# S5 mixer: signs and decays made behind the scan, one transfer for a Toeplitz matrix, a norm factor in step order

## The chip, the cores and the metric

The program runs on one core of a Trainium2 chip. The metric is device time in microseconds (us) from the start to the end of one launch, the median of several runs; lower is better. TensorE is called PE below (PEld is its weight load), VectorE DVE, ScalarE ACT, GpSimd POOL, and SyncE, which issues all the transfers here, SP.

## The reference

The reference sends 256 tokens of 1024 features through two blocks in 32-bit floats. The first block has two layers: a mixer of a convolution and a retention, then a feed-forward part; and a second layer whose mixer is the bidirectional S5 that this change touches, then a feed-forward part. The second block is a mix of three attentions and a gated feed-forward part. Of the S5 mixer, this is what matters:

```python
def _mixer_s5(h, lam_re, ..., w_glu_a, w_glu_b):
    # 64 groups of 16 channels each drive a 64-dim complex diagonal state, per direction
    ug = u.reshape(bsz, seq, 64, 16)
    ...
    for direction in (0, 1):
        bu = einsum('sgc,gpc->sgp', us, bb[direction])              # complex
        h = associative_scan(_s5_combine, (a, bu), reverse=direction == 1)
        y = y + einsum('sgp,gcp->sgc', h_re, c_re) - einsum('sgp,gcp->sgc', h_im, c_im)
    y = y + d_skip * u
    z = gelu(y)
    return (z @ w_glu_a) * sigmoid(z @ w_glu_b)
```

The input `h` of the mixer is the root-mean-square norm of `x`, scaled and shifted by a modulation.

## The kernel before

Features lie on partitions and the 256 tokens in the free dimension. A dense layer takes its weights in pieces of 1 MB: `load` (L296) transfers a piece into one of four tiles of the tag `w`, `split` (L301) makes a high part of it on ACT (L314) and a low part on DVE (L315) into the tags `hi` and `lo` (two tiles each), and `lin` multiplies by three matmuls (L319 to L321). While the first layer's feed-forward part runs, `s5_tables` builds the S5 tables and writes them to memory: `Wd` (into the states), `Vd` (out of them) and `Kd` (a Toeplitz matrix of the taps inside a chunk).

The second layer's mixer begins with the norm: `rms` sums squares, takes the inverse root, and `spread` (L369) puts the factor of each token on all partitions, as two matmuls into PSUM. `modulated` (L1150 on DVE, L1151 on ACT) multiplies and shifts, and turns token order into step order: the 256 tokens are 32 chunks `j` of 8 steps `s`, stored as `(j s)`, and the stage wants `(s j)`.

`s5` then works on eight rows `ip` of eight groups each. For a row:

- `load(ip)` transfers `Wt` and `Vt` (two transfers of 512 KB each) and, for even rows, the Toeplitz matrix `Mt` (1 MB for two rows) as eight transfers of 16 partitions each (L1018). It also makes the small factors: `dm`, the decays with a zero at each chunk row's start (L1022 on POOL, L1026 on ACT), and `sg`, the signed sines (L1024, L1025 on ACT). The rooms that the tables use are borrowed: `wplace`, `vplace` and `mplace` name tags whose tiles the dense layers also use. `dm` and `sg` have two tiles each, so those of row `ip + 2` take the room of row `ip`.
- `chunk_states(ip)` multiplies the input by `Wt` on PE (L1039), copies the result `X` to SBUF on ACT (L1041) and transposes it on PE (L1045).
- `scan(ip)` has six operations on DVE: L1058, L1059 and L1060 turn the states, L1061 is the scan along the chunks with `dm`, L1065 and L1066 turn back; POOL adds the halves (L1067, L1068) into `S`.
- `outputs(ip)` adds up `Mt` (L1079) and `S` with `Vt` (L1081) on PE; after an odd row ACT copies the result to `Y` (L1114).

The loop has a look-ahead of two rows for the loads and of one row for the states:

```python
tabs = {ip: load(ip) for ip in range(self.ahead)}              # ahead = 2
pT = {ip: chunk_states(ip, tabs[ip]) for ip in range(self.skew)}  # skew = 1
for ip in range(8):
    if ip + self.ahead < 8:
        tabs[ip + self.ahead] = load(ip + self.ahead)
    if ip + self.skew < 8:
        pT[ip + self.skew] = chunk_states(ip + self.skew, tabs[ip + self.skew])
    S = scan(pT.pop(ip), tabs[ip])
    ...
    outputs(ip, S, tabs.pop(ip), pY)
```

`finish` adds the skip term (L1094), applies the activation (L1095) and splits the result; the two dense layers `glu_a` and `glu_b` follow, four pieces each. The low part of their first pieces (L315) is tied behind the last scan on DVE; the high part on ACT (L314) isn't tied to anything.

The order of instructions on each engine and on the transfer queue isn't the program's order. A planner makes it while the program is built: it goes by priority, which is program order, among what its own model of the times holds to be ready. On the chip each engine then runs its queue strictly in that order. `X`, `S` and the two products of L1065 and L1066 share one tag of five tiles, and a tile is handed on when its last reader is done.

Of the kernel before, what the change touches and what calls it, by code (L numbers as in the profile page):

```python
# [12 lines left out]
ALU = mybir.AluOpType  # L13
# [161 lines left out]
class K:  # L175
# [185 lines left out]
            st.add(x)  # L361
        return st.get()

    def spread(self, cols, tag=None):

        n = cols.shape[1]
        pb = self.ps(tag or self.pb_tag)[:, :128 * n]
        for b in range(n):
            self.nc.tensor.matmul(pb[:, 128 * b:128 * b + 128], cols[:, b:b + 1].to_broadcast([128, 128]), self.ident, start=True, stop=True)  # L369
        return pb  # L370

    def rms(self, x, st=None):

        ms = self.sumsq(x, st)
        return self.spread(self.rsqrt_eps(ms[:, :, 0]))

    def gained(self, x, g):

# [573 lines left out]
    def s5(self, x, u, fill, need, between, each, l=1):  # L952

        nc, v = self.nc, self.nc.vector

        H2 = self.sb([128, 16, 8, 16])
        for ih in range(2):
            for s4 in range(2):
# [3 lines left out]
                o = H2[:, 8 * ih:8 * ih + 8, 4 * (1 - s4):8 - 4 * s4][:, :, ::-1].rearrange("p i s c -> p s i c")  # L962
                src = ps.rearrange("p (s i c) -> p s i c", s=4, i=8)
# [6 lines left out]
        for i4 in range(4):  # L970
# [3 lines left out]
            o = U[:, 4 * i4:4 * i4 + 4].rearrange("p i x -> p (i x)")  # L974
# [6 lines left out]
        def tab(shape, tag):  # L981
            return self.tabs[tag].tile(shape, F32, name=self.name(tag), tag=tag)
# [11 lines left out]
        def wide(tag, place, ip):  # L994

            t = room(tag, place)
            src = self.Wd if tag == "Wt" else self.Vd
            out = []
            for i in range(2):
                o = t[:, 1024 * i:1024 * i + 1024]  # L1000
                nc.sync.dma_start(o, src[2 * ip + i].rearrange("p g n -> p (g n)"))
                out.append(o)
            return out
# [4 lines left out]
        mt = []  # L1008

        def load(ip):  # L1010
            Wt = wide("Wt", self.wplace[ip], ip)
            Wt = [w.rearrange("p (e r d q) -> p e r d q", e=4, r=2, d=2) for w in Wt]
            dm = tab([128, 2, 8, 32], "dm")
            if ip % 2 == 0:

                mt.append(room("Mt", self.mplace[ip // 2]).rearrange("p (l e i n) -> p l e i n", e=4, i=4, n=16))
                for s in range(8):
                    nc.sync.dma_start(mt[-1][16 * s:16 * s + 16].rearrange("c l e i n -> c (l e i n)"),  # L1018
                                      self.Kd[ip // 2][:, s:s + 8].rearrange("c l e n -> c (l e n)"))
            Mt = mt[-1][:, :, :, 2 * (ip % 2):2 * (ip % 2) + 2]  # L1020
            Et = self.E[:, :, 8 * ip:8 * ip + 8]
            nc.gpsimd.memset(dm[:, :, :, 0], 0.0)  # L1022
            sg = tab([128, 2, 8, 32], "sg")
            nc.scalar.copy(sg[:, 0], Et[:, 1])  # L1024
            nc.scalar.mul(sg[:, 1], Et[:, 1], -1.0)  # L1025
            (nc.scalar.copy if self.dm_act else nc.gpsimd.tensor_copy)(dm[:, :, :, 1:], self.rho[:, None, 8 * ip:8 * ip + 8, None].to_broadcast([128, 2, 8, 31]))  # L1026
            Vt = wide("Vt", self.vplace[ip], ip)
            Vt = [w.rearrange("p (e r n) -> p e r n", e=4, r=2) for w in Vt]
            return Wt, Vt, Mt, Et[:, 0], sg, dm

        def chunk_states(ip, tabs):

# [16 lines left out]
        Z, Tt = (self.ps(q).rearrange("p (r g j) -> p r g j", r=2, j=32) for q in ("fa", "fp"))  # L1049
        v.memset(Z[:, :, :, 0], 0.0)  # L1050

        def scan(pT, tabs):
            cs, sg, dm = tabs[3:]
            both = lambda a: a[:, None].to_broadcast([128, 2] + list(a.shape[1:]))

            t = [self.sb([128, 2, 8, 32], tag="q2") for _ in range(2)]
            a, b = t[0][:, :, :, 1:], t[1][:, :, :, 1:]
            tt(a, pT[:, :, :, 0:31], both(cs[:, :, 1:]), op=ALU.mult)  # L1058
            tt(b, pT[:, ::-1, :, 0:31], sg[:, :, :, 1:], op=ALU.mult)  # L1059
            tt(Z[:, :, :, 1:], a, b, op=ALU.add)  # L1060
            v.tensor_tensor_scan(fl(Tt), fl(dm), fl(Z), 0.0, op0=ALU.mult, op1=ALU.add)  # L1061
            S = self.sb([128, 2, 8, 32])
            fw, bw = slice(0, 64), slice(64, 128)
            t = [self.sb([128, 2, 8, 32]) for _ in range(2)]
            tt(t[0], Tt, both(cs), op=ALU.mult)  # L1065
            tt(t[1], Tt[:, ::-1], sg[:, ::-1], op=ALU.mult)  # L1066
            nc.gpsimd.tensor_tensor(S[fw], t[0][fw], t[1][fw], op=ALU.add)  # L1067
            nc.gpsimd.tensor_tensor(S[bw][:, :, :, ::-1], t[0][bw], t[1][bw], op=ALU.add)  # L1068
            return S

        def outputs(ip, S, tabs, pY):
            _, Vt, Mt = tabs[:3]
            for i in range(2):
                for k in range(3):
                    for e in range(4):
                        o = pY[32 * e:32 * e + 32, 2 * (ip % 2) + i]
                        kw = dict(start=k == 0, stop=k == 2, tile_position=(0, 32 * e))
                        if k == 0:
                            nc.tensor.matmul(o, U[:, 2 * ip + i, 32 * e:32 * e + 32], Mt[:, :, e, i], **kw)  # L1079
                        else:  # L1080
                            nc.tensor.matmul(o, S[:, k - 1, 4 * i + e], Vt[i][:, e, k - 1], **kw)  # L1081

# [16 lines left out]
        if self.warm:  # L1099
            nc.scalar.activation(self.sb([128, 1]), self.half, AF.Gelu_apprx_tanh)  # L1100
        tabs = {ip: load(ip) for ip in range(self.ahead)}
        pT = {ip: chunk_states(ip, tabs[ip]) for ip in range(self.skew)}
        for ip in range(8):
            if ip + self.ahead < 8:
                tabs[ip + self.ahead] = load(ip + self.ahead)
            if ip + self.skew < 8:
                pT[ip + self.skew] = chunk_states(ip + self.skew, tabs[ip + self.skew])
            S = scan(pT.pop(ip), tabs[ip])
            scanned = {mybir.EngineType.DVE: self.last(mybir.EngineType.DVE)}
            if ip % 2 == 0:  # L1110
                pY = self.ps(self.y_tag[ip // 2 % 2]).rearrange("p (i n) -> p i n", i=4)
            outputs(ip, S, tabs.pop(ip), pY)
            if ip % 2:
                nc.scalar.copy(Y[:, :, 2 * ip - 2:2 * ip + 2].rearrange("p t i c -> p i t c"), pY.rearrange("p i (t c) -> p i t c", c=16))  # L1114
            if ip == 3 + self.defer:
                with self.held(mybir.EngineType.DVE):
                    finish(0)
            self.behind(fill, self.rates[2][1])
# [7 lines left out]
        for j in range(4):  # L1126
            pa, pb = self.pair(), self.pair("fp")
# [10 lines left out]
            for c in range(2):  # L1138
                n = 2 * j + c
# [5 lines left out]
    def modulated(self, x, r, g, shift):  # L1145

        u = self.sb([128, 2, 8, 4, 32])
        for c in (0, 2, 4, 6, 1, 3, 5, 7):
            h, by = self.sb([128, 8, 32]), lambda a: a.rearrange("p (j s) -> p s j", s=8)
            self.nc.vector.scalar_tensor_tensor(h, by(x[:, c]), g[:, c:c + 1], by(r), op0=ALU.mult, op1=ALU.mult)  # L1150
            self.nc.scalar.activation(u[:, c % 2, :, c // 2], h, AF.Identity, bias=shift[:, c:c + 1])  # L1151
        return u

# [399 lines left out]
    def build(self, stop=None):  # L1553
        nc = self.nc
        with ExitStack() as es:
# [8 lines left out]
            x = self.keep([128, 8, T], "x")  # L1564
# [29 lines left out]
            with self.phase(s4=self.m4, ap=1, cv=self.ncv):  # L1594
                self.mark("norm0")
                h = self.normed(x, self.rms(x), self.modg(0, 1, 0), self.modv(0, 0))
                self.mark("mixer0")
                st = Sums(self)
# [8 lines left out]
            with self.phase(s4=4):  # L1607
                self.mark("norm0f")
                h = self.normed(x, self.rms(x, st), self.modg(0, 4, 1), self.modv(0, 3))
                self.mark("ffn0")  # L1610
                st = Sums(self)
# [8 lines left out]
            self.rate = self.rates[2]  # L1620
            with self.phase(s8=4):
                self.mark("norm1")
                u = self.modulated(x, self.rms(x, st), self.modg(1, 1, 0), self.modv(1, 0))
                self.mark("s5")
                def between():
                    nonlocal mem
                    tab_pools.close()
                    self.mkv, self.memh = mem_pools.enter_context(rpool("mkv", 1)), memh_pool.__enter__()
                    mem = Fill(self.memory())
                    ACT = mybir.EngineType.Activation  # L1630
                    self.after(mem, self.memat[0], ACT, self.last(ACT))

                mem, mem_pools, memh_pool = None, ExitStack(), rpool("memh", 1)
                st = Sums(self)
                self.s5(x, u, ada, lambda: need(1, 2), between, lambda j: st.add(x))
                need(1, 4)
                glu_end = self.last(mybir.EngineType.PE)
                self.dump("x3", x)
# [4 lines left out]
            with self.phase(s4=4):  # L1643
                self.mark("norm1f")
                r = self.rms(x, st)
                if self.mempace:
                    self.after(mem, self.memat[1], mybir.EngineType.PE, glu_end)
                h = self.normed(x, r, self.modg(1, 4, 1), self.modv(1, 3))
# [58 lines left out]
```

## Time and profile before

| | |
|---|---|
| median of 3 runs | 1232.63 us (1230.88 to 1236.48) |
| the profiled execution | 1235.0 us, of which its span 1233.2 us |
| busy share of the span | PE 95%, PEld 90%, DVE 72%, ACT 50%, POOL 8% |
| granted TensorE clock, mean | 0.971 of full speed |

A row of the timeline gives the start in us from the span's start, the duration, the engine (SPq is SP's queue), the line, the operation with its output and input, how many instructions were merged into it, and in brackets how long the engine had been idle before it and what released it. Buffer numbers are left out of names, so `s`, `at`, `fp` are all tiles of a tag. A transfer in SP's rows is its issue, not its movement.

### The profile page before, as it was taken

The page shows a single profiled execution, that of the slowest core. Times are in us where ns is not written, and L with a number is a line of the kernel's source. Part 1 is how long each engine was busy: PE and PEld are TensorE (multiplying, and loading weights), DVE is VectorE, ACT ScalarE, POOL GpSimd, SP SyncE. Part 2 cuts the span into 40 slices and gives each one's busy share as a digit, 9 for nine tenths or more (in the row PEclk, how much of TensorE's full clock was granted, in tenths as well). Part 3 has the DMA queues.
Part 4 walks back from the last instruction along what each step waited for, and adds up shares of the span by engine and source line. Part 5 has one row for each costly group of instructions (what it writes and reads, how often), then busy time and mean ns, then how long its engine had stood idle before and what let it go on. Part 6 is the DMA issues. An engine that isn't in the chain of part 4 may idle for free. (4 is left out here: it accounts for less than half of the span.)

```text
span 1233.2 us, 25410 instructions
## 1 busy us (share of the span) xinstructions
PE 1168.6 (95%) x10482; PEld 1110.2 (90%) x10482; DVE 890.2 (72%) x1813; ACT 613.5 (50%) x1218; POOL 104.0 (8%) x122
## 2 busy tenths in 40 slices
PE   6899897999999965799999999999999999999998
PEld 3688686999999954699999999999999999999998
DVE  7879887889888867766766656686666686666564
ACT  3577243655555643546444445573455545454441
POOL 0078321000000005100000000000000000000000
PEclk9899997999999978799999999999999999999999
DMA  9879886788888999354465655443454454555541
GB/s 348 337 304 334 295 293 200 236 271 286 284 295 269 297 274 343 123 186 162 159 262 206 223 187 167 167 171 103 137 172 137 152 173 157 187 187 172 193 157 60
DMA packets 64091, 267.29 MB, mean 217 GB/s; under 512 B 10196, under 2 KB 29028, under 8 KB 36840
## 3 DMA queue, kind: packets, MB, share of 16 engines
q1 hardware_dynamic: 63976, 265.68, 62.7%
q8 instruction: 82, 1.34, 0.4%
q14 instruction: 33, 0.27, 0.1%
HBM read 246.85 MB, written 18.81 MB: 215 GB/s over the span
## 5 line engine op out<-in xcount | busy, mean ns | idle before, releaser
L315 DVE TENSOR_TENSOR lo<-w,hi 128x512 fp32r<-128x512 f32 (+1 forms) x640 | 428.0, 714 | 148.7 <-ACT hi L314 148.1
L314 ACT ACTIVATE hi<-w 128x512 fp32r<-128x512 f32 (+1 forms) x640 | 358.3, 625 | 337.1 <-PE mm L320 120.1
L319 PE MATMUL mm<-h,hi 128*128 128x256 f32 x1328 | 380.9, 287 | 0.4 <-ACT h L398 0.3
L320 PE MATMUL mm<-h,hi 128*128 128x256 f32 x1328 | 378.8, 285 | 1.2 <-DVE h L399 1.1
L321 PE MATMUL mm<-h,lo 128*128 128x256 f32 x1328 | 379.9, 286 | 0.1
L319 PEld LDWEIGHTS mm<-h,hi 128*128 128x128 f32 x1328 | 256.0, 193 | 7.4 <-issue 3.4
L320 PEld LDWEIGHTS mm<-h,hi 128*128 128x128 f32 x1328 | 256.0, 193 | 2.8 <-DVE h L399 1.5
L321 PEld LDWEIGHTS mm<-h,lo 128*128 128x128 f32 x1328 | 255.8, 193 | 2.7 <-issue 1.6
L321 PE MATMUL at<-s,lo 128*128 128x256 f32 x720 | 204.4, 284 | 1.4 <-DVE lo L315 1.4
L319 PE MATMUL at<-s,hi 128*128 128x256 f32 x720 | 204.8, 284 | 0.0
L320 PE MATMUL at<-s,hi 128*128 128x256 f32 x720 | 204.1, 284 | 0.0
L321 PEld LDWEIGHTS at<-s,lo 128*128 128x128 f32 x720 | 137.9, 192 | 2.2 <-DVE lo L315 1.8
L319 PEld LDWEIGHTS at<-s,hi 128*128 128x128 f32 x720 | 138.0, 192 | 1.8 <-issue 1.4
L320 PEld LDWEIGHTS at<-s,hi 128*128 128x128 f32 x720 | 138.0, 192 | 0.6 <-issue 0.6
L439 PE MATMUL fa<-wa,crep 128*32 128x256 f32 x704 | 56.1, 424 | 6.9 <-DMA wa<-in_ada_dram 3.7
L537 POOL TENSOR_TENSOR s<-s,cv 128x256 f32<-128x256 f32 x60 | 49.9, 864 | 39.1 <-ACT cv L536 39.0
L439 PEld LDWEIGHTS fa<-wa,crep 128*32 128x32 f32 x704 | 22.6, 118 | 27.0 <-DMA wa<-in_ada_dram 5.9
L320 PE MATMUL fp<-h,hi 128*128 128x256 f32 x144 | 41.6, 289 | 0.9 <-DVE h L315 0.9
L319 PE MATMUL fp<-h,hi 128*128 128x256 f32 x144 | 41.4, 288 | 0.0
L321 PE MATMUL fp<-h,lo 128*128 128x256 f32 x144 | 41.4, 287 | 0.0
L929 ACT COPY Wt<-fp 128x512 f32<-128x512 f32 x32 | 18.6, 581 | 44.7 <-PE fp L928 41.2
L536 ACT ACTIVATE cv<-ap,s 128x256 f32<-128x256 f32 x60 | 29.5, 506 | 17.2 <-POOL s L537 16.4
(439 smaller groups left out, 1826.0 us busy)
## 6 DMA issues: line engine op xcount, KB each, us to landing
w<-in_fc_dram SPq DMA_DIRECT2D x64, 1024.0 KB, 5.0
wa<-in_ada_dram SPq DMA_DIRECT2D x44, 1024.0 KB, 6.6
w<-in_w_in_dram SPq DMA_DIRECT2D x38, 1024.0 KB, 4.9
w<-in_w_gate_dram SPq DMA_DIRECT2D x11, 1024.0 KB, 4.8
w<-in_w_up_dram SPq DMA_DIRECT2D x11, 1024.0 KB, 4.9
Vd<-V SPq DMA_DIRECT2D x16, 512.0 KB, 6.5
w<-in_w_out_dram SPq DMA_DIRECT2D x8, 1024.0 KB, 6.2
Wd<-Wt SPq DMA_DIRECT2D x16, 512.0 KB, 5.3
```

What stands on the lines that cost most here:

```text
L314: self.nc.scalar.activation(hi, h, AF.Copy)
L315: self.nc.vector.tensor_tensor(lo, h, hi.bitcast(F32), op=ALU.subtract)
L319: mm(ps, sh, mh, start=start, stop=False, skip_group_check=True)
L320: mm(ps, sh, ml, start=False, stop=False, skip_group_check=True)
L321: mm(ps, sl, mh, start=False, stop=stop, skip_group_check=True)
L439: nc.tensor.matmul(ps[32 * q:32 * q + 32], self.crep[:, 2 * k + k2], w[:, n:n + 256], start=k == 0 and k2 == 0, stop=k == 3 and k2 == 1, t ...
L536: nc.scalar.mul(t, src, w)
L537: nc.gpsimd.tensor_tensor(acc[:, ch], acc[:, ch], t, op=ALU.add)
L929: nc.scalar.copy(W[:, :, k], pt.rearrange("p (e x) -> p e x", e=4))
```

## The change

Three edits. First, `load(ip)` no longer makes `sg` and `dm`; a new function `factors(ip)` does, on the same engines. It is called for rows 0 and 1 ahead of the loop, and for row `ip + 2` right after `scan(ip)`, which is the last reader of the room that they take. Second, `Mt` is filled by one transfer on all 128 partitions in place of eight on 16 each; its source pattern has the dimensions step (8), channel (16) and run (2048 elements). Third, the norm's factor is put into PSUM in step order: the matmuls of `spread` write with a stride of 32 elements, and `modulated` reads it in a row, where it read it with a stride of 8 elements.

```diff
-    def spread(self, cols, tag=None):
+    def spread(self, cols, tag=None, steps=False):
...
-            self.nc.tensor.matmul(pb[:, 128 * b:128 * b + 128], cols[:, b:b + 1].to_broadcast([128, 128]), self.ident, start=True, stop=True)
+            o = pb.rearrange("p (s j) -> p j s", s=8)[:, 16 * b:16 * b + 16] if steps else pb[:, 128 * b:128 * b + 128]
+            self.nc.tensor.matmul(o, cols[:, b:b + 1].to_broadcast([128, 128]), self.ident, start=True, stop=True)
...
         def load(ip):
...
-            dm = tab([128, 2, 8, 32], "dm")
             if ip % 2 == 0:
...
-                for s in range(8):
-                    nc.sync.dma_start(mt[-1][16 * s:16 * s + 16].rearrange("c l e i n -> c (l e i n)"),
-                                      self.Kd[ip // 2][:, s:s + 8].rearrange("c l e n -> c (l e n)"))
+                src = self.Kd[ip // 2]
+                nc.sync.dma_start(mt[-1].rearrange("p l e i n -> p (l e i n)"),
+                                  bass.AP(tensor=src.tensor, offset=src.offset, ap=[[256, 8], [3840, 16], [1, 2048]]))
...
-            nc.gpsimd.memset(dm[:, :, :, 0], 0.0)
-            sg = tab([128, 2, 8, 32], "sg")
-            nc.scalar.copy(sg[:, 0], Et[:, 1])
-            nc.scalar.mul(sg[:, 1], Et[:, 1], -1.0)
-            (nc.scalar.copy if self.dm_act else nc.gpsimd.tensor_copy)(dm[:, :, :, 1:], self.rho[:, None, 8 * ip:8 * ip + 8, None].to_broadcast([128, 2, 8, 31]))
...
+        def factors(ip):
+
+            Et, rho = self.E[:, :, 8 * ip:8 * ip + 8], self.rho[:, None, 8 * ip:8 * ip + 8, None]
+            sg, dm = tab([128, 2, 8, 32], "sg"), tab([128, 2, 8, 32], "dm")
             nc.scalar.copy(sg[:, 0], Et[:, 1])
             nc.scalar.mul(sg[:, 1], Et[:, 1], -1.0)
+            nc.gpsimd.memset(dm[:, :, :, 0], 0.0)
+            nc.scalar.copy(dm[:, :, :, 1:], rho.to_broadcast([128, 2, 8, 31]))
+            return Et[:, 0], sg, dm
...
+        fac = {ip: factors(ip) for ip in range(2)}
...
-            S = scan(pT.pop(ip), tabs[ip])
+            S = scan(pT.pop(ip), fac.pop(ip))
...
+            if ip + 2 < 8:
+                fac[ip + 2] = factors(ip + 2)
             outputs(ip, S, tabs.pop(ip), pY)
...
-            self.nc.vector.scalar_tensor_tensor(h, by(x[:, c]), g[:, c:c + 1], by(r), op0=ALU.mult, op1=ALU.mult)
+            self.nc.vector.scalar_tensor_tensor(h, by(x[:, c]), g[:, c:c + 1], r.rearrange("p (s j) -> p s j", s=8), op0=ALU.mult, op1=ALU.mult)
...
-                u = self.modulated(x, self.rms(x, st), self.modg(1, 1, 0), self.modv(1, 0))
+                u = self.modulated(x, self.rms(x, st, True), self.modg(1, 1, 0), self.modv(1, 0))
```

## Rows read from the trace of the kernel before

**Rows 1.** Page, part 2: busy tenths of PE in 40 slices of the span.

```profile
PE   6899897999999965799999999999999999999998
```

**Rows 2.** Windows of the S5 stage: window, length, then busy time per engine, clock, DMA share, GB/s.

```profile
455.00:482.00 27.00, 18.65 (x416) 14.88 (x415) 24.10 (x33) 9.82 (x22) 13.05 (x15) 0.87 1.03 344
482.00:497.00 15.00, 4.53 (x69) 2.96 (x68) 6.97 (x10) 5.85 (x13) 4.49 (x4) 0.74 0.64 229
497.00:510.00 13.00, 8.23 (x146) 6.46 (x142) 12.76 (x25) 3.83 (x8) 5.40 (x4) 0.76 0.16 42
```

**Rows 3.** Timeline of DVE, rows 5 to 7 of the loop.

```profile
482.56 1.23 DVE L1061 TENSOR_TENSOR_SCAN fp<-dm,fa 128x512 f32<-128x512 f32 x1
...
486.75 1.23 DVE L1061 TENSOR_TENSOR_SCAN fp<-dm,fa 128x512 f32<-128x512 f32 x1
488.08 0.69 DVE L1065 TENSOR_TENSOR s<-fp,E 128x512 f32<-128x512 f32 x1
496.56 0.69 DVE L1066 TENSOR_TENSOR s<-fp,sg 128x512 f32<-128x512 f32 x1 [7.79 <-PE at L1045]
```

**Rows 4.** Timeline of PE, the same stretch.

```profile
475.16 2.08 PE L1039 MATMUL mm<-Wt,s 128*32 128x128 f32 x62
...
479.46 1.06 PE L1039 MATMUL mm<-Wt,s 128*32 128x128 f32 x32
...
495.34 1.11 PE L1045 MATMUL at<-ident,s 128*128 128x128 f32 x4 [8.22 <-ACT s L1041]
```

**Rows 5.** Timeline of ACT, the same stretch.

```profile
481.20 0.56 ACT L1041 COPY s<-mm 128x512 f32<-128x512 f32 x1
...
491.52 2.19 ACT L314 ACTIVATE hi<-w 128x512 fp32r<-128x512 f32 x4 [9.15 <-DMA w<-in_glu_a_dram]
493.61 0.59 ACT L1026 COPY dm<-rho 128x496 f32<-128x496 f32 x1
...
494.73 0.56 ACT L1041 COPY s<-mm 128x512 f32<-128x512 f32 x1
```

**Rows 6.** Timeline of SP's queue, end of the loop.

```profile
470.74 11.16 SPq L1018 DMA_DIRECT2D Mt<-Kd  x8
482.35 0.35 SPq L1216 DMA_DIRECT2D m<-in_mem_dram  x1
482.90 0.35 SPq L298 DMA_DIRECT2D w<-in_glu_a_dram  x1
```

**Rows 7.** Waits of SP from 415 to 520 us: total, times, longest.

```profile
SPq L1018 <- DMA Wt<-Wd: 10.5, 8, 2.7
```

**Rows 8.** Windows as in rows 2, by what the transfers carry.

```profile
478.00:484.00 6.00, 4.12 (x104) 3.28 (x108) 5.76 (x8) 2.96 (x7) 5.35 (x6) 1.00 0.96 194
464.00:478.00 14.00, 10.59 (x240) 8.56 (x232) 11.89 (x17) 4.82 (x11) 6.31 (x9) 0.83 1.04 409
426.00:432.00 6.00, 6.00 (x53) 6.00 (x52) 1.13 (x3) 1.50 (x3) 0.00 (x0) 1.00 1.06 161
```

**Rows 9.** By source line: issues of L1018 (ns), landings of L298 from 455 us.

```profile
L1018 SPq DMA_DIRECT2D Mt<-Kd x24: 302/318/932, 422.6 to 481.6; - x24
...
DMA to landing us min/median/max: 4.9/8.0/10.5
```

**Rows 10.** Waits of DVE from 455 to 503 us.

```profile
DVE q L1058 <- PE at L1045: 3.7, 3, 1.9
```

**Rows 11.** By source line: ns min/median/max, first and last start.

```profile
L1150 DVE SCALAR_TENSOR_TENSOR s<-x,modg,at x8: 659/668/685, 442.4 to 446.5; 128x256 f32<-128x256 f32 x8
...
L397 DVE SCALAR_TENSOR_TENSOR s<-x,modg,at x24: 441/478/481, 34.9 to 580.6; 128x256 f32<-128x256 f32 x24
...
L1141 DVE SCALAR_TENSOR_TENSOR x<-s,hgate,x x8: 716/732/765, 530.3 to 566.4; 128x256 f32<-128x256 f32 x8
```

**Rows 12.** Timeline of PE, the norm's spread ahead of the loop.

```profile
441.15 1.22 PE L369 MATMUL at<-ident,s 128*128 128x128 f32 x4 [2.22 <-DVE s L349]
```

**Rows 13.** Waits of PE from 515 us to the end: all of them.

```profile
PE mm L320 <- DVE h L384: 0.2, 1, 0.2
```

More of the change, by code (lines that the diff above doesn't have):

```diff
@@ L368, in spread, with rms @@
         for b in range(n):
-            self.nc.tensor.matmul(pb[:, 128 * b:128 * b + 128], cols[:, b:b + 1].to_broadcast([128, 128]), self.ident, start=True, stop=True)
+            o = pb.rearrange("p (s j) -> p j s", s=8)[:, 16 * b:16 * b + 16] if steps else pb[:, 128 * b:128 * b + 128]
+            self.nc.tensor.matmul(o, cols[:, b:b + 1].to_broadcast([128, 128]), self.ident, start=True, stop=True)
         return pb
-    def rms(self, x, st=None):
+    def rms(self, x, st=None, steps=False):
         ms = self.sumsq(x, st)
-        return self.spread(self.rsqrt_eps(ms[:, :, 0]))
+        return self.spread(self.rsqrt_eps(ms[:, :, 0]), steps=steps)
     def gained(self, x, g):
@@ L1012, in load @@
             Wt = [w.rearrange("p (e r d q) -> p e r d q", e=4, r=2, d=2) for w in Wt]
-            dm = tab([128, 2, 8, 32], "dm")
             if ip % 2 == 0:
                 mt.append(room("Mt", self.mplace[ip // 2]).rearrange("p (l e i n) -> p l e i n", e=4, i=4, n=16))
-                for s in range(8):
-                    nc.sync.dma_start(mt[-1][16 * s:16 * s + 16].rearrange("c l e i n -> c (l e i n)"),
-                                      self.Kd[ip // 2][:, s:s + 8].rearrange("c l e n -> c (l e n)"))
+                src = self.Kd[ip // 2]
+                nc.sync.dma_start(mt[-1].rearrange("p l e i n -> p (l e i n)"),
+                                  bass.AP(tensor=src.tensor, offset=src.offset, ap=[[256, 8], [3840, 16], [1, 2048]]))
             Mt = mt[-1][:, :, :, 2 * (ip % 2):2 * (ip % 2) + 2]
-            Et = self.E[:, :, 8 * ip:8 * ip + 8]
-            nc.gpsimd.memset(dm[:, :, :, 0], 0.0)
-            sg = tab([128, 2, 8, 32], "sg")
+            Vt = wide("Vt", self.vplace[ip], ip)
+            Vt = [w.rearrange("p (e r n) -> p e r n", e=4, r=2) for w in Vt]
+            return Wt, Vt, Mt
+        def factors(ip):
+            Et, rho = self.E[:, :, 8 * ip:8 * ip + 8], self.rho[:, None, 8 * ip:8 * ip + 8, None]
+            sg, dm = tab([128, 2, 8, 32], "sg"), tab([128, 2, 8, 32], "dm")
             nc.scalar.copy(sg[:, 0], Et[:, 1])
             nc.scalar.mul(sg[:, 1], Et[:, 1], -1.0)
-            (nc.scalar.copy if self.dm_act else nc.gpsimd.tensor_copy)(dm[:, :, :, 1:], self.rho[:, None, 8 * ip:8 * ip + 8, None].to_broadcast([128, 2, 8, 31]))
-            Vt = wide("Vt", self.vplace[ip], ip)
-            Vt = [w.rearrange("p (e r n) -> p e r n", e=4, r=2) for w in Vt]
-            return Wt, Vt, Mt, Et[:, 0], sg, dm
+            nc.gpsimd.memset(dm[:, :, :, 0], 0.0)
+            nc.scalar.copy(dm[:, :, :, 1:], rho.to_broadcast([128, 2, 8, 31]))
+            return Et[:, 0], sg, dm
         def chunk_states(ip, tabs):
@@ L1050, in s5, with scan @@
         v.memset(Z[:, :, :, 0], 0.0)
-        def scan(pT, tabs):
-            cs, sg, dm = tabs[3:]
+        def scan(pT, fac):
+            cs, sg, dm = fac
             both = lambda a: a[:, None].to_broadcast([128, 2] + list(a.shape[1:]))
@@ L1071, in outputs @@
         def outputs(ip, S, tabs, pY):
-            _, Vt, Mt = tabs[:3]
+            _, Vt, Mt = tabs
             for i in range(2):
```

## The prediction

> **What bounds the kernel now.** The page's second part comes first, because PE is busy nearly everywhere: the reader is to look for slices where it isn't, and the longest run of them after the start is slices 14 to 16, about 430 to 525 us [rows 1]. That is the S5 stage. The windows then say which engine sets the pace inside it. From 455 to 482 us DVE is busy 24.10 of 27.00 us, PE 18.65, ACT 9.82: the six operations of a row on DVE are the bound. From 482 to 497 us every engine is under half busy, DVE at 6.97 of 15.00. From 497 to 510 us DVE is full again [rows 2]. So one hole stands in a stage that DVE otherwise sets.
>
> The timelines of three engines name the hole's chain. DVE ends L1065 of row 6 at 488.77 us and starts L1066 only at 496.56, 7.79 us idle, released by a transpose on PE [rows 3]. L1066 reads nothing that this transpose makes; it needs a tile of the shared tag, the one that row 7's `X` holds until it is transposed. That transpose waited 8.22 us for ACT's copy of `X` [rows 4]. Its source was ready early: row 7's products on PE were done at 480.5 us (479.46 + 1.06) [rows 4]. ACT copied row 6's `X` at 481.20 and then stood 9.15 us at L314, which makes the high part of the first `glu_a` piece and waited for its transfer; `dm`, `sg` and `X` of row 7 are queued behind it [rows 5]. SP's queue says why the piece came so late. It was issued at 482.90, behind eight transfers of `Mt` that took 11.16 us to issue from 470.74 on [rows 6]. An issue by itself takes 0.318 us [rows 9], so 8.6 us of the 11.16 were waits; over the stage, SP's largest wait is L1018 for the landing of earlier transfers, eight times, 10.5 us in all [rows 7]. After the stage PE waits 0.2 us in all until the end [rows 13], so what the stage saves or loses reaches the end in full.
>
> **The change part by part.**
>
> *One transfer for `Mt`.* Four times eight issues become four single ones: 28 x 0.318 = 8.9 us less of SP, with the waits between them. That SP time lies on the path in one place only, ahead of `glu_a`. Behind the one issue at 470.74 us, `m` and `glu_a` stand next. `glu_a` needs a tile of the tag `w`. Ten tiles of it are asked for in the order Wt1, Vt1, Wt2, Wt3, Wt6, Wt7, Vt7, `m`, `glu_a`, `glu_b`; by the order in which the rooms come free, `glu_a` gets that of Wt6, free when row 6's products end at 477.24 us (475.16 + 2.08; PE makes those of loop rows 5 and 6 in one go) [rows 4]. So the issue moves from 482.90 to about 477.5 us, no earlier. Landing takes 4.9 us at the least, 8.0 in the median here [rows 9]: 482.4 to 485.5 us. If ACT's order stays as it is, ACT needs 3.77 us from the landing to the end of `X` (491.52 to 494.73 + 0.56) [rows 5], and PE's transpose 1.11 [rows 4]: 487.3 to 490.4 us. DVE is ready at 488.77 [rows 3]. The remaining wait is then 0 to 1.6 us of today's 7.79; I take 0.5. **Gain 7.3 us, bounds 6.2 and 7.8.**
>
> Whether the bytes themselves go faster is a second question. The stretch that carries mostly `Mt` runs at 194 GB/s, the one of `Wt` and `Vt` on 128 partitions at 409, both with the transfer engines full (share 0.96 and 1.04); another `Mt` stretch has 161 [rows 8]. 1.05 MB takes 5.4 us at the one rate and 2.6 at the other, 2.8 us apart for each of four matrices. No row shows the new pattern. Bounds: no gain, or 11.2 us of transfer time, none of which is on the path before `glu_a`. It decides which end of the landing range holds, nothing more, and has no term of its own.
>
> [...]
>
> *`sg` and `dm` behind the scan.* Nothing is added or removed: per row two copies, one activation and a memset, and `dm` alone takes 0.59 us on ACT [rows 5]. All wait for `scan(ip)` before and after, since they take its room. What moves is their priority: `X` of row `ip + 1` now stands ahead of the factors of row `ip + 2`. In the trace DVE waits 3.7 us in three places for transposes that follow such copies [rows 10]; the first, 1.9 us, is the loop's start, which the edit doesn't touch. The other 1.8 us are the upper bound; the lower is nothing, since DVE is the bound and a copy that was late elsewhere cost it nothing. No row separates the share that ACT's order caused; I take a little under half. **Gain 0.8 us, bounds 0 and 1.8.** What hides ACT's 1.68 us for `dm`, `sg` and `X` of a row (493.61 to 495.29) [rows 5] is DVE, full while ACT is busy 9.82 of 27.00 us [rows 2]; without that cover it would show once per row.
>
> The planner may also order `glu_a`'s L314 anew, since its own model sees a shorter transfer queue. `X` of row 7 may come ahead of it, and then the residual 0.5 us goes too. Or L314 moves further ahead; that is a rival below.
>
> *Norm factor in step order.* L1150 takes 668 ns with both inputs strided, L397 478 ns with neither: at most 8 x 0.19 = 1.5 us [rows 11]. But `x` stays strided in SBUF, and L1141, whose strides are in SBUF alone (one read and the write), takes 732 ns [rows 11]. This is the nearer row: the stride that stays explains the whole excess. I take nothing. Against it stand the matmuls of `spread`, 1.22 us [rows 12], whose output becomes strided. No row has PE writing so; from nothing to the factor by which strides slow DVE (732/478 = 1.5, so 0.6 us). I take nothing here too. **0 us, bounds a gain of 1.5 and a loss of 0.6.**
>
> [...]
>
> **The sum.** 7.3 + 0.8 + 0 = 8.1 us. The profiled execution took 1235.0 us, 1.8 more than its span of 1233.2; it lies 2.4 above the median of 1232.63. A shift of 8.1 us gives 1226.9 us on its scale and 1224.5 on that of the median, which I predict.
>
> **The rivals.**
>
> 1. *The hole shrinks only.* If the new pattern moves no faster than the old 194 GB/s, `Mt`, `m` and `glu_a` share a backlog still. Transfers of 2.6 us each for `m` and `glu_a` behind a matrix of 5.4 us that begins when Vt7 ends, at 478 us at the latest [rows 8], land at 488.6. Row 7's transpose then ends at 493.5, 4.7 us after DVE is ready: gain 3.1 + 0.8, about 1228.7. For it: the transfer engines are full all through the loop. Against it: SP no longer halts between issues, so earlier loads also come sooner. [...]
>
> 2. *The wait reappears elsewhere, no change.* DVE gets past row 6, but the first low parts (L315) behind the last scan then wait for the pieces, or a borrowed room comes free late. Then the 8 us are given back before `glu` begins: 1232.6. Against it: the piece's room is free at 477 us, and ACT has over 10 us after that.
>
> 3. *Slower: ACT's queue is worse.* The planner, seeing the pieces land earlier in its model, puts L314 of both pieces ahead of row 6's `X`, while on the chip they land as late as today. Then row 6 waits too: 4.2 us more of DVE work comes after the hole (the distance of the scans of rows 5 and 6, 482.56 to 486.75) [rows 3], and 2.2 more for the second piece: 1236.8 to 1239.0. It decides if `glu_a` lands later than about 480 us and L314 stands ahead of the copy at 481.20 [rows 5]. Against it: the piece's room comes from row 6's own products, so the copy is ready before the transfer can begin.
>
> **How the numbers follow.** A difference under 0.5% (6.2 us) is about what a measurement of this kernel can't tell from no change. The forecast (a gain of 6.2 to 10.6 us) gets 0.60, a larger gain (more waits of DVE go, the norm gets its 1.5 us) 0.06, rival 1 (2 to 6.2 us) 0.17, rival 2 0.11, rival 3 0.06. Faster is 0.60 + 0.06 = 0.66; rivals 1 and 2 and the milder half of rival 3 are the same, 0.31; slower 0.03. For 8 in 10, the range runs from 1221 (all upper bounds together, 7.8 + 1.8 + 1.5 = 11.1) to 1233 (rival 2); it leaves out rival 3 and a part of the largest gains. The likeliest case's own range is 1222 to 1226.4.
>
> **What would show each step.** Right: on ACT no wait for `glu_a` over 2 us; DVE's idle time ahead of L1066 of row 6 gone, scans 4.2 to 5.7 us apart to the last; SP's issue of `glu_a` at 475 to 478 us; L1018 with four issues; L1150 near 668 ns and L369 near 1.2 us. Wrong: L314 of `glu_a` standing on ACT ahead of an `X` copy with a long wait, a stretch of `Mt` at under 250 GB/s with `glu_a` landing past 487 us, or L369 doubled. The prediction fails most easily on the planner: its new order can't be read from this trace.

## The result and the profile after

The changed kernel took 1252.46 us in the median of four runs (1248.74 to 1253.43), the kernel before 1232.74 beside it: a ratio of 1.0151 with an interval of 1.0119 to 1.0182. It is 19.7 us slower; 8.1 us faster was forecast, and 1233 was the end of the range. The profiled execution took 1253.08 us with a span of 1251.3, 18.1 more than the span before.

DVE's timeline of the changed kernel, where it stood longest (start, length, operation, and in brackets the idle time before it). L1069 and L1070 were L1065 and L1066.

```profile
470.80 0.69 DVE L1070 TENSOR_TENSOR s<-fp,sg 128x512 f32<-128x512 f32 x1 [9.05 <-PE at L1049]
...
479.47 0.68 DVE L1062 TENSOR_TENSOR q<-at,E 128x496 f32<-128x496 f32 x1 [3.38 <-PE at L1049]
...
495.82 0.69 DVE L1069 TENSOR_TENSOR s<-fp,E 128x512 f32<-128x512 f32 x1
514.23 0.69 DVE L1070 TENSOR_TENSOR s<-fp,sg 128x512 f32<-128x512 f32 x1 [17.71 <-PE at L1049]
```

Two things happened. The hole of row 6 did not close but grew from 7.79 us [rows 3] to 17.71. And an early hole of 9.05 us stands ahead of L1070 of row 1 (rows are counted from 0), where the kernel before has none. The same L1070 of row 6 begins at 514.23 against 496.56 [rows 3], 17.7 us later, and that is nearly the whole of the span's 18.1. Half is lost on each side. DVE ended the operation ahead of the late hole at 496.51 against 488.77, 7.7 us later. The stage's norm had begun 1.9 us earlier (`spread` on PE at 439.25 against 441.15 [rows 12]), which can't be laid to the edits: in the profiles of the kernels below that change no code ahead of the norm, its modulation begins anywhere from 440.5 to 445.4 us. So 9.6 us went early; the late hole is 9.9 longer.

PE's timeline of the changed kernel shows what each hole waited for: the early ones for `Wt`, the late one for ACT.

```profile
467.39 2.26 PE L1043 MATMUL mm<-Wt,s 128*32 128x128 f32 x32 [12.15 <-DMA Wt<-Wd]
469.57 1.12 PE L1049 MATMUL at<-ident,s 128*128 128x128 f32 x4
473.72 2.27 PE L1043 MATMUL mm<-Wt,s 128*32 128x128 f32 x32 [3.03 <-DMA Wt<-Wd]
...
513.00 1.12 PE L1049 MATMUL at<-ident,s 128*128 128x128 f32 x4 [19.34 <-ACT s L1045]
```

PE stood 12.15 us for row 3's `Wt`. The transpose of row 2's `X`, for which DVE waits at row 1's L1070, is queued behind those products, and so the stall on a load reached DVE. At the end the chain is the old one [rows 4, 5], only longer. ACT's timeline of the changed kernel:

```profile
489.54 0.59 ACT L1121 COPY s<-at 128x512 f32<-128x512 f32 x1
509.18 2.19 ACT L314 ACTIVATE hi<-w 128x512 fp32r<-128x512 f32 x4 [19.06 <-DMA w<-in_glu_a_dram]
...
512.39 0.56 ACT L1045 COPY s<-mm 128x512 f32<-128x512 f32 x1
```

L314 stands ahead of row 7's `X` as before: PE had its products done at 488.27 us (L1043, 487.21 + 1.06), and ACT copied them only behind L314, at 512.39. The factors' new place in the program changed nothing in this order. The wait went from 9.15 us [rows 5] to 19.06. SP's timeline of the changed kernel (start of the first issue, length of the group, issues):

```profile
421.13 1.72 SPq L1018 DMA_DIRECT2D Mt<-Kd  x2
...
423.87 0.60 SPq L1018 DMA_DIRECT2D Vt<-Kd  x1
424.52 13.96 SPq L1002 DMA_DIRECT2D Wt<-Wd  x4
...
453.04 12.25 SPq L1002 DMA_DIRECT2D Wt<-Wd  x2
...
483.85 0.60 SPq L1018 DMA_DIRECT2D Mt<-Kd  x1
485.11 0.34 SPq L1223 DMA_DIRECT2D m<-in_mem_dram  x1
486.36 0.33 SPq L298 DMA_DIRECT2D w<-in_glu_a_dram  x1
```

The issue of a matrix now takes 0.60 us where eight took up to 11.16 [rows 6], as forecast. But SP isn't free: its waits moved to the issues of `Wt` behind the matrices. SP's waits of the changed kernel from 415 to 520 us (total, times, longest):

```profile
SPq L1002 <- DMA Mt<-Kd: 19.8, 2, 11.7
...
SPq L1002 <- DMA Vt<-Kd: 11.6, 1, 11.6
```

These 31.4 us in three waits are for matrices to land. The fourth matrix is issued at 483.85 us, where its eight parts began at 470.74 before [rows 6], and `glu_a` at 486.36, where it was 482.90 before and about 477.5 in the forecast. And what SP issues lands late: three matrices (the third in a room of tag `Vt`) stand in the queue by 424.5 us, and the first `glu_a` piece needs 22.8 us from its issue to 509.18, where it needed 8.6 before [rows 5, 6]. Windows of the changed kernel, columns as in [rows 2]:

```profile
424.00:444.00 20.00, 13.81 (x110) 13.35 (x110) 8.66 (x25) 7.24 (x13) 0.00 (x0) 0.88 1.04 169
...
462.00:466.00 4.00, 0.00 (x0) 0.00 (x0) 0.00 (x0) 0.00 (x0) 0.20 (x2) 0.50 0.47 140
500.00:510.00 10.00, 0.00 (x0) 0.00 (x0) 0.00 (x0) 0.82 (x2) 0.00 (x0) 0.50 0.54 188
```

The first of these windows lies where the matrices are backed up. The kernel before had, in the same window:

```profile
424.00:444.00 20.00, 15.23 (x120) 14.76 (x118) 8.15 (x26) 7.06 (x15) 0.00 (x0) 0.85 1.03 231
```

The transfer engines are all busy in both (1.04 and 1.03), and yet 169 GB/s are moved in place of 231. Late in both waits the engines are about half busy (0.47 and 0.54) while PE and DVE do nothing, and TensorE's granted clock lies at 0.50. Full engines at a low rate first (1.04, 169 GB/s), and half busy engines at the end (0.54), is the picture to remember. The norm, finally, is where it was: its modulation by source line (ns, shortest, median, longest) and its `spread` on PE, both of the changed kernel.

```profile
L1157 DVE SCALAR_TENSOR_TENSOR s<-x,modg,at x8: 662/668/682, 440.5 to 444.6; 128x256 f32<-128x256 f32 x8
```

```profile
439.25 1.22 PE L370 MATMUL at<-ident,s 128*128 128x128 f32 x4 [2.22 <-DVE s L349]
```

668 ns as before [rows 11], and 1.22 us as before [rows 12]; DVE's first modulation starts 1.26 us after `spread` began in both (440.51 and 442.41).

### The profile page after: what moved, and what is told of

The parts are those of the page before. It is cut to its first block, busy times and chain, and to the rows that moved or that the text cites. A ratio compares the mean times of both kernels' runs of the same rounds, so it can differ in the third digit from the quotient of the medians.

```text
span 1251.3 us, 25377 instructions
## 1 busy us (share of the span) xinstructions
PE 1166.4 (93%) x10482; PEld 1107.2 (88%) x10482; DVE 888.8 (71%) x1813; ACT 613.6 (49%) x1218; POOL 104.1 (8%) x122
## 5 line engine op out<-in xcount | busy, mean ns | idle before, releaser
L315 DVE TENSOR_TENSOR lo<-w,hi 128x512 fp32r<-128x512 f32 (+1 forms) x640 | 427.2, 711 | 147.5 <-ACT hi L314 146.8
L314 ACT ACTIVATE hi<-w 128x512 fp32r<-128x512 f32 (+1 forms) x640 | 358.3, 625 | 344.6 <-PE mm L320 120.5
```

Source lines behind the costliest of these rows:

```text
L314: self.nc.scalar.activation(hi, h, AF.Copy)
L315: self.nc.vector.tensor_tensor(lo, h, hi.bitcast(F32), op=ALU.subtract)
```

## The experiments

**Which edit it was.** Each way round: the change with the eight transfers put back, and the kernel before with the single transfer alone.

```diff
 # e1_eight: the changed kernel; e2_one_only: the same lines the other way, on the kernel before
-nc.sync.dma_start(mt[-1]..., bass.AP(..., ap=[[256, 8], [3840, 16], [1, 2048]]))
+for s in range(8):
+    nc.sync.dma_start(mt[-1][16 * s:16 * s + 16]..., self.Kd[ip // 2][:, s:s + 8]...)
```

> The changed kernel with the eight transfers of 16 partitions put back for Mt; the factors behind the scan and the norm factor in step order stay. Theory A (the one transfer of Mt is what costs: it holds half of the transfer engines for long and everything queued behind it comes late): the 20 us go, 1230 to 1235 us, DVE's waits in the loop as in the kernel before (7.8 us ahead of L1066 of row 6). Theory B (moving the factors gave the planner another order that is worse on the chip): still 1245 us or more.

> The kernel before with the one transfer of Mt as its only edit. Theory A: 1248 to 1254 us, PE waiting for Wt of row 2 (12 us) and ACT for the first glu_a piece (19 us) as in the changed kernel. Theory B: 1230 to 1235 us.

With the eight transfers back: 1235.78 us against 1234.49, ratio 1.0003 (0.9986 to 1.0020). The single transfer alone: 1252.62, ratio 1.0146 (1.0124 to 1.0169), which is the changed kernel's. So the transfer is the whole loss, and the other two edits are worth nothing that these total times can show (the interval leaves room for some 2 us). DVE's waits in the first of these kernels (total, times, longest):

```profile
DVE s L1070 <- PE at L1049: 6.6, 1, 6.6
...
DVE q L1062 <- PE at L1049: 3.9, 3, 1.9
```

The old hole is back at 6.6 us, and the three waits that the moved factors might have shortened still come to 3.9 (3.7 before [rows 10]). In the kernel with the single transfer alone DVE's and then ACT's waits read:

```profile
DVE s L1066 <- PE at L1045: 23.1, 2, 15.5
```

```profile
ACT hi L314 <- DMA w<-in_glu_a_dram: 16.8, 1, 16.8
```

Both holes are there, without either of the other edits. (The wait that two of the expectations put at `Wt` of row 2 is, by the order of PE's products, that for row 3.)

**The transfer by itself.** A kernel with nothing but transfers of 1 MB into 128 partitions, twice in each pattern, then ahead of other loads.

```diff
+plain: 128 rows of 2048   eight: [16 rows] x8   one: [[256, 8], [3840, 16], [1, 2048]]
+outer: [[3840, 16], [256, 8], [1, 2048]], other tile layout (channel outermost)
```

> Transfers alone, no S5 work: 1 MB to 128 partitions as plain rows, as eight transfers of 16 partitions in order and in another order, as the one transfer (step, channel, run) and with the channel outermost, each twice by itself; then each ahead of four plain 1 MB loads, and three of a kind ahead of two. [...] Theory D (the pattern is not slow by itself, only its place in the queue): one transfer is no slower than eight.

DVE's timeline of this kernel, second of each pair (the wait in brackets is that for the transfer, a few tenths shorter than the transfer itself): plain, eight, one, channel outermost.

```profile
11.31 0.16 DVE L54 TENSOR_TENSOR acc<-acc,m 128x1 f32<-128x1 f32 x1 [4.50 <-DMA m<-in_w_dram]
...
31.18 0.16 DVE L54 TENSOR_TENSOR acc<-acc,m 128x1 f32<-128x1 f32 x1 [9.34 <-DMA m<-in_kd_dram]
...
74.81 0.16 DVE L54 TENSOR_TENSOR acc<-acc,m 128x1 f32<-128x1 f32 x1 [11.53 <-DMA m<-in_kd_dram]
...
89.47 0.16 DVE L54 TENSOR_TENSOR acc<-acc,m 128x1 f32<-128x1 f32 x1 [6.66 <-DMA m<-in_kd_dram]
```

Windows of the same kernel while such transfers move bytes, in the same order (window, length, DVE, POOL, clock, DMA share, GB/s):

```profile
8.00:11.00 3.00, 0.00 (x0) 0.00 (x0) 1.00 0.80 328
23.00:29.00 6.00, 0.00 (x0) 0.00 (x0) 1.00 1.05 145
53.00:61.00 8.00, 0.00 (x0) 0.00 (x0) 1.00 0.52 121
77.00:81.00 4.00, 0.00 (x0) 0.00 (x0) 1.00 0.96 231
```

The one transfer is the slowest of all: 12.0 us against 9.5 for the eight, 7.0 with the channel outermost and 5.0 for plain rows. (At the prediction's 194 GB/s [rows 8] the eight would have taken 5.4. Issued in another order, 0, 4, 1, 5 and so on, they are waited for 9.1 and 8.4 us.) While the bytes move, the one keeps the engines about half busy (share 0.52) at 121 GB/s, the eight keep them full (1.05) at 145. The channel-outermost transfer reads the same bytes from the same place at 231, so the source alone doesn't make the one slow. And the one holds up what stands behind it. With four 1 MB loads behind the matrix, DVE waited in the same timeline for the matrix, first of the eight, then of the one:

```profile
114.77 0.16 DVE L54 TENSOR_TENSOR acc<-acc,m 128x1 f32<-128x1 f32 x1 [9.33 <-DMA m<-in_kd_dram]
...
140.30 0.16 DVE L54 TENSOR_TENSOR acc<-acc,m 128x1 f32<-128x1 f32 x1 [14.68 <-DMA m<-in_kd_dram]
```

The loads cost the eight nothing (9.33 us, as alone) and the one 3 us more (14.68 against 11.53). Windows of the same kernel behind the one, while the matrix was under way and towards the end of the loads:

```profile
130.00:138.00 8.00, 0.00 (x0) 0.00 (x0) 1.00 1.05 161
146.00:149.00 3.00, 0.16 (x1) 0.00 (x0) 1.00 0.50 210
```

With loads behind it the engines are full while the matrix is under way (1.05), and at the end they are half busy (0.50) at half of the 426 GB/s that loads alone reach in this run (98 to 100 us). Yet the last loads land 2.47 us apart (145.04 to 149.97 us on DVE), as they do behind plain rows (2.49, 97.27 to 104.72). So by these numbers, and as an estimate, half of their bytes had been moved earlier, beside the matrix, and no load was complete ahead of it. Full first and half busy at the end is also the pattern of the changed kernel (1.04, then 0.54). The last of the four loads landed 19.8 us after the first issue behind eight transfers, 24.7 behind one and 14.9 behind plain rows. Three matrices in a row and two loads took 29.9, 38.8 and (channel outermost) 21.2 us. Those 8.9 us more of the one over the eight are near the 9.6 that the changed kernel lost ahead of the late hole, behind three such matrices.

**Why the one is slow.** Again transfers alone: 1 MB into 32 partitions, split over 8 or 16 outermost parts, and into 16 partitions the same way, to set the number of parts apart from the partitions written.

```diff
+[[4 * 8192 + 64, 8], [8192, 4], [1, 8192]]    # 32 partitions, 8 outermost
+[[2 * 8192 + 64, 16], [8192, 2], [1, 8192]]   # 32 partitions, 16 outermost
+[[2 * 16384 + 64, 8], [16384, 2], [1, 16384]] # 16 partitions, 8 outermost
+[[16384 + 64, 16], [1, 16384]]                # 16 partitions, 16 outermost
```

> Transfers alone again, to part the number of transfer engines from the partitions they meet on. 1 MB each, twice each: to 32 partitions as 8 x 4 rows and as 16 x 2 rows, to 16 partitions as 8 x 2 rows and as 16 rows. Theory P (the rate goes by which partitions are being written, whatever number of engines writes them): both forms to 32 partitions take about the same, some 6 to 7 us, and both forms to 16 about the same, some 10 to 12 us. Theory H (half of the engines means half of the rate): the forms with 8 outermost take about twice as long as those with 16.

DVE's timeline of that kernel, one row of each pair in this order:

```profile
18.62 0.15 DVE L55 TENSOR_TENSOR acc<-acc,m 32x1 f32<-32x1 f32 x1 [7.49 <-DMA m<-in_w_dram]
...
35.01 0.15 DVE L55 TENSOR_TENSOR acc<-acc,m 32x1 f32<-32x1 f32 x1 [7.81 <-DMA m<-in_w_dram]
...
60.69 0.15 DVE L55 TENSOR_TENSOR acc<-acc,m 16x1 f32<-16x1 f32 x1 [12.49 <-DMA m<-in_w_dram]
...
84.78 0.15 DVE L55 TENSOR_TENSOR acc<-acc,m 16x1 f32<-16x1 f32 x1 [11.66 <-DMA m<-in_w_dram]
```

Twice the parts gain nothing at 32 partitions (7.5 and 7.8 us) and 7% at 16; half the partitions cost 49 to 67%. Here the time goes with the partitions written. And 8 outermost parts alone don't make 1 MB take 12 us, since into 32 partitions they take 7.5; the rows there are longer (32 KB against 8 KB), which no run sets apart. The single transfer writes 128 partitions and is still waited for as long as one into 16 (11.53 against 11.66 and 12.49 us). Over these waits 1.05 MB make 91 GB/s for the single transfer and 90 and 84 into 16 partitions: near each other; in the window above, while its bytes move, the single transfer has 121. No trace shows in which order it writes its partitions, so why it is as slow as a transfer into 16 is not shown.

**The matrix without its pattern.** The changed kernel, with the one transfer reading plain rows of a weight.

```diff
-    bass.AP(tensor=src.tensor, offset=src.offset, ap=[[256, 8], [3840, 16], [1, 2048]]))
+    self.I["fc1_1"][ip // 2].rearrange("p k n -> p (k n)"))
```

> The changed kernel with Mt filled by one transfer of plain rows (128 rows of 8 KB in a row, from a weight array), so Mt holds other numbers than the Toeplitz matrix; everything else as in the changed kernel, the order on ACT too. It has the one issue and full-rate bytes, which the prediction had assumed. Theory A: the step of the prediction that failed is the transfer alone, so this comes near the predicted 1224.5 us: 1222 to 1228 us, glu_a landing by 486 us. Rival E: the planner's order holds L314 ahead of row 7 with a late piece anyway: 1230 us or more.

1225.55 us against 1233.88, ratio 0.9934 (0.9921 to 0.9947): 8.3 us, where 8.1 was forecast for the change itself. SP's timeline of this kernel, then ACT's:

```profile
466.48 0.33 SPq L1017 DMA_DIRECT2D Mt<-in_fc_dram  x1
...
475.54 0.33 SPq L298 DMA_DIRECT2D w<-in_glu_a_dram  x1
```

```profile
480.75 2.19 ACT L314 ACTIVATE hi<-w 128x512 fp32r<-128x512 f32 x4
```

`glu_a` is issued at 475.54 and L314 begins without a wait; DVE has no hole at row 6. The source is another array too, but the single transfer alone, which was slow above, read an input array as well, so it is the pattern. The path was read rightly; what failed is the transfer's own time.

**The late hole without touching a transfer.** L314 of `glu_a` is tied behind row 7's copy of `X` on ACT. This goes on three kernels: the changed one with eight transfers, the kernel before, and the changed one as it is.

```diff
                 pT[ip + self.skew] = chunk_states(ip + self.skew, tabs[ip + self.skew])
+                copied = self.last(mybir.EngineType.Activation)
 ...
             scanned = {mybir.EngineType.DVE: self.last(mybir.EngineType.DVE)}
+            scanned[mybir.EngineType.Activation] = copied
```

> As e1_eight, and the high parts of the first two glu pieces on ACT are tied behind row 7's copy of X. Theory A with the chain of the prediction (ACT's L314 ahead of row 7's X makes the hole): the wait ahead of L1066 of row 6 goes, ACT does row 7's factors and X at once, 1223 to 1227 us. Rival C (the pieces' landing sets the end of the stage, whichever work stands ahead of L314): 1230 to 1235 us, with DVE waiting at L315 for the high parts instead.

> The kernel before with one edit: the high parts of the first two glu pieces on ACT are tied behind row 7's copy of X. If moving the factors and the norm factor are worth nothing, as e1_eight says, this alone gives what e4_eight_held gave: 1225 to 1228 us, ratio 0.993 to 0.995. Rival: the hold works only together with the moved factors, then over 1230 us.

> The changed kernel with its one transfer and the same hold on ACT. It divides the loss. Theory A2: about 10 us of it is the wait for Wt of row 2 early in the loop, which the hold doesn't touch, and the rest is the late glu_a piece; with the hold only a part of the second comes back, since DVE then waits at L315 for the same landing: 1238 to 1246 us. Rival: all of the late loss comes back, 1234 us or less; or none, 1250 us.

With eight transfers 1226.47 us, ratio 0.9937 (0.9922 to 0.9951); on the kernel before 1226.94, ratio 0.9945 (0.9932 to 0.9957). The hole was an order on ACT as much as a late transfer. ACT's timeline of the first:

```profile
486.81 0.56 ACT L1045 COPY s<-mm 128x512 f32<-128x512 f32 x1
489.86 2.19 ACT L314 ACTIVATE hi<-w 128x512 fp32r<-128x512 f32 x4 [2.48 <-DMA w<-in_glu_a_dram]
```

`X` goes first, and the wait for `glu_a` has shrunk to 2.48 us, off DVE's path. On the changed kernel the tie gives 1244.63 us, ratio 1.0081 (1.0065 to 1.0097): 0.7% of the 1.5% come back. PE's waits there, and then DVE's:

```profile
PE mm L1043 <- DMA Wt<-Wd: 16.2, 3, 12.6
PE at L1083 <- DMA Mt<-Kd: 9.0, 1, 9.0
```

```profile
DVE s L1070 <- PE at L1049: 9.7, 1, 9.7
...
DVE s L1070 <- PE at L1085: 7.5, 1, 7.5
```

The early wait stays, and at the end the fourth matrix itself is late: PE's outputs wait 9.0 us for it, and DVE behind them, at L1070, where L315 was expected.

**Place in the queue.** In the changed kernel the third matrix is issued ahead of the `Wt` of rows 3 and 4. Here each matrix is tied behind the `Wt` of its own row.

```diff
+                with self.held(mybir.EngineType.SP):
                     nc.sync.dma_start(mt[-1]...
```

> The changed kernel with each transfer of Mt tied, on the queue, behind the Wt of its own row, so that the third matrix no longer stands ahead of the Wt of rows 3 and 4 (in the changed kernel it does; with eight transfers it didn't). It parts the price of the slow transfer from that of its place. If the place makes the early wait: the 12 us for Wt of row 3 shrinks to under 4 us and the total comes to 1238 to 1246 us, the late wait for glu_a staying. If two slow matrices ahead of it are enough: 1248 to 1254 us as in the changed kernel.

1254.86 us, ratio 1.0169 (1.0138 to 1.0199): no better. The third matrix was now issued at 457.07 us. PE's timeline of this kernel, at rows 3 and 6:

```profile
459.43 0.65 PE L1044 MATMUL mm<-Wt,s 128*32 128x128 f32 x16 [2.29 <-DMA Wt<-Wd]
460.61 0.64 PE L1044 MATMUL mm<-Wt,s 128*32 128x128 f32 x16 [0.53 <-DMA Wt<-Wd]
...
486.33 2.23 PE L1044 MATMUL mm<-Wt,s 128*32 128x128 f32 x32 [9.67 <-DMA Wt<-Wd]
```

The wait for row 3's `Wt` did shrink, to 2.8 us, so two matrices ahead of it don't make it. But the third now stands ahead of row 6's `Wt`, and PE waits 9.67 us there; its waits for `Wt` come to 15.4 us, 16.2 in the changed kernel. The matrix's place decides which load comes late, and not how much is lost.

**A faster pattern in the kernel.** On the changed kernel with eight transfers and the tie: one transfer with the channel outermost, and the layouts of its producers turned to suit.

```diff
-            Wn = work([128, 2, 4, 8, 16], "W")
+            Wn = work([128, 2, 4, 16, 8], "W").rearrange("p k e c s -> p k e s c")
...
-        H2 = self.sb([128, 16, 8, 16])
+        H2 = self.sb([128, 16, 16, 8])
...
+                   bass.AP(..., ap=[[3840, 16], [256, 8], [1, 2048]]))
```

> As e4_eight_held, but Mt comes in one transfer with the channel (16) outermost; the partition order of the states' input and of Wt is changed to match, by strided writes on DVE and ACT. Its transfer took 7.0 us by itself and 4.5 in a row of three, against 9.5 and 7.7 for eight. If DVE bounds the loop once the hold is there: as e4_eight_held, 1224 to 1228 us, with glu_a landing some 5 us earlier. If the loop or the pieces still wait for transfers: 1220 to 1223 us. Rival: the strided writes cost more than that, over 1229 us.

1229.28 us, ratio 0.9969 (0.9957 to 0.9981): faster than before, but not as fast as the tie alone, and just inside the rival's "over 1229". Writes in the turned layouts cost more. By source line, in this kernel:

```profile
L966 DVE COPY s<-at x2: 1089/1091/1093, 452.0 to 454.4; 128x512 f32<-128x512 f32 x2
```

The same copy takes 692 ns with the tie on the kernel before, but it comes twice only. More lies in the tables that are built ahead of the stage: two operations on `W` (L922 and L923, 16 of each) have medians of 1176 and 1158 ns, where they have 686 and 684 with eight transfers and the tie, and the norm's modulation begins at 446.99 us in place of 442.21. From there to L1098 this kernel takes 50.1 us, against 51.7 with eight transfers and the tie and 49.6 with the tie alone, one execution of each, so what the faster pattern is worth inside the loop can't be told. The fastest that compute the reference's numbers are the tie alone (1226.94) and the tie with the two small edits (1226.47), not to be told apart.

## Why the prediction was wrong

**The step that failed** is the second question on the one transfer for `Mt`, whether the bytes go faster. It read: "Bounds: no gain, or 11.2 us of transfer time, none of which is on the path before `glu_a`." Both halves fell. A loss was not among the bounds, and the runs measured one: 12.0 us for 9.5 alone, 24.7 for 19.8 with four loads behind, 38.8 for 29.9 in a row of three. And the transfers are on the path: row 3's `Wt` queues behind three matrices, PE waits 12.15 us for it, and DVE behind PE; later `glu_a` queues behind the fourth. The step on SP fell with it: it kept the last matrix's issue at 470.74 us and moved that of `glu_a` to 477.5, but SP stood 31.4 us for the first three matrices, and the issues came at 483.85 and 486.36. The rows held a part of the warning: the stretch of backlogged `Mt` moved 161 GB/s with all engines busy (1.06) [rows 8]. The other part, a share of 0.52 while the single transfer alone moves bytes, stood in no row. With half of the share, half of the 161 would be some 80 GB/s, or 1.05 MB in 13 us, an estimate from these two. That it comes near the 12.0 measured is in part luck: while it moved bytes the one transfer had 121 GB/s.

**The rival that came nearest.** Rival 1 had the new pattern move no faster than the old. But it priced it at 194 GB/s, the rate of the eight, where the single transfer alone had 121 at a share of 0.52, and it followed it into the last matrix only, for a gain of 3.9 us. It had half of the mechanism, a backlog, and neither its size nor its place: four matrices are slow, and the first three lie ahead of loads that PE is about to need. Rival 3 had the direction, slower, by another mechanism.

**What held.** The chain of the late hole held in every link: taking ACT's order out of it gives 0.55% (the tie on the kernel before), taking the transfer out gives 0.66%. The term of 7.3 us is that of the plain rows, 8.3 us in all against the 8.1 forecast, with the issue at 475.54 (475 to 478 forecast); from the norm's first modulation to `finish` (L1150 to L1094, there L1156 to L1097) that kernel takes 51.8 us where the kernel before takes 59.4, the hole and no more. In the changed kernel it never came, as `glu_a` landed 17.7 us later than before. The moved factors measured nothing where 0.8 us was taken (bounds 0 and 1.8): ACT's order around the hole stayed, and the waits stayed at 3.9 us. The norm's 0 was right to the nanosecond, 668 and 668, and `spread` takes 1.22 us before and after: strided PSUM output cost TensorE nothing here. And taking the stride from DVE's PSUM input gained nothing, which fits the argument that the stride of `x` in SBUF accounts for the excess, without showing it. Rival 3 did not come about, since the planner's order around the hole is unchanged. The sign named for a wrong forecast, L314 ahead of an `X` copy with a long wait and `glu_a` past 487 us, is what the trace shows. One reading of a row was off and touched nothing: in the window of [rows 7] SP's largest single wait is L298's for L315, 23.1 us, after the issues in question.

**What stays open** is why the one transfer is slow by itself (the order of its writes, or what keeps the engines' share at 0.52), and how the late half divides. `glu_a` was issued 3.5 us later and took 14.2 more to land, while DVE itself came 7.7 later. How much of the 14.2 is the matrix, and how much `m` and the tables queued with it, no run separates.

## What to carry to other kernels

Fewer transfers are not a wider transfer. Before several are merged, time both patterns alone and ahead of the loads that follow: here that small run had the answer (12.0 against 9.5 us, 24.7 against 19.8). And where an instruction that waits for a late load stands ahead of a critical copy on the same engine (L314 ahead of `X` on ACT, 9.15 us), tying it behind the copy is the cheaper cure: two lines gave 0.55% with no transfer touched.

## What the runs showed of the hardware

A transfer into all 128 partitions was slower than eight into 16 each, and as slow as 1 MB into 16 partitions (12.0, 9.5 and some 12 to 12.6 us), while the same bytes with the 16 channels outermost took 7.0: the shape of a transfer counts, not only how many partitions it fills. And the single transfer holds back whole loads behind it: alone it keeps the engines about half busy (share 0.52) and with loads behind it they are full (1.05), and still the first load was waited for 2.1 us after the matrix and did not land before, and the fourth landed 24.7 us after the first issue, where it took 19.8 behind eight transfers. The loads slowed the single transfer in turn, from 11.5 us to 14.7.
